# A list-scheduled two-layer block: new durations in the scheduler, and weight loads further ahead in the transfer queue

## The chip, the cores and the metric

The kernel runs on one core of a Trainium2 chip. The metric is device time in microseconds of one execution. The core's engines are TensorE (PE, matmuls; its weight loads are a row of their own, PEld), VectorE (DVE), ScalarE (ACT), GpSimd (POOL) and SyncE (SP), which here does nothing but issue all transfers (DMAs) in one order. Each engine executes its own instructions strictly in the order of the program.

## The reference, cut to what matters

Two layers over 1024 latent tokens and 256 context tokens, width 1024. In each, a conditioning vector gives scale, shift and gate (`w_ada`, 1024 x 3072), the normalised input goes through one projection (`w_in`, 1024 x 3600), four head groups work on slices of it, and an output projection closes the layer. The context shares the weights and feeds the latents only through the final states of the DeltaNet scan.

```python
for l in range(DEPTH):                                   # 2
    mod = silu(c) @ w_ada[l] + b_ada[l]                  # shift, scale, gate; the same with c_ctx
    h  = rmsnorm(x,  norm_g[l]) * (1 + scale) + shift
    hc = rmsnorm(xc, norm_g[l]) * (1 + scale_c) + shift_c
    if l % 2 == 1: h = to_col_major(h)
    p, pc = h @ w_in[l], hc @ w_in[l]                    # last layer: context needs group A only
    o_ctx, s_f, s_b = gdn_bidir(pc[..., :A_COLS], 0, 0, ...)
    o_lat, _, _     = gdn_bidir(p[..., :A_COLS], s_f, s_b, ...)
    y = mixer_output(o_lat, p, ...) # norm, conv3, conv31 + LayerNorm, spatial gate; each times silu(gate)
    x = x + gate * (y @ w_out[l])   # the context likewise in layer 0
return rmsnorm(x, final_g)
```

`gdn_bidir` works in chunks of 64 tokens: pair matrices of a chunk, the inverse of a triangular matrix, then a scan over chunks in both directions that carries a 64 x 64 state for each of 4 heads.

## The kernel before

**Dense work.** Each fp32 product is made of three matmuls in a rounded type (`mm3`): the weight tile is split into a high part (ScalarE CAST, `w<-r` or `u<-r`) and a low part (VectorE TENSOR_TENSOR `w<-r,w`), the input likewise (`hh`, `hl`). A projection takes 128 output columns at a time: 24 matmuls of 512 latent columns (or 256 context columns) fill one PSUM bank `mm`, of which there are three; an eviction then frees it. `dense` (its inner function `pump`) runs the pipeline of weights: load a raw tile `r` (512 KB, two buffers), split it, use it. While a raw tile is not yet split its buffer is taken.

**The program is recorded, then ordered.** All calls go to `Program.record` and `add`, which give each operation its dependences, an estimated duration (`estimate`; for a transfer a constant on SP), and a priority: its place in the recorded program plus the current `boost` (smaller is earlier). `schedule` then runs through estimated time and gives each engine, whenever it is free, the ready operation with the smallest priority; that fixes every engine's order, SP's too. Operations given with two engines (`either`: evictions, casts and scale-and-shift on ScalarE or VectorE) get their engine there, by which would be done first. So a changed duration moves instructions on all engines and from one engine to the other, though the set of operations stays the same. Priority offsets already exist: the scan stands 800 places ahead (`AHEAD_SCAN`), the splits in `pump` 600 (`AHEAD_SPLIT`), the DeltaNet preparation 300.

**Stages of the time.** The start: `c` arrives, eight `w_ada` tiles of 1 MB (`whh`, `whl`) feed the modulation, after each second one a slice of the context's `hh`, `hl` is ready (0 to 43 us). Then layer 0: context projections mixed with the making of the latents' `hh0` (to 164 us), latent projections, the context scan, the latent scan (440 to 590 us), the output projection with layer 1's `hh1`, token tile by token tile (690 to 810 us). Layer 1: projections, the context's inverse and scan (960 to 1000 us), the latents' pair matrices and inverse, the latent scan (1110 to 1200 us), the output projection. Of the names below, `mm` are dense PSUM banks, `sc` and `ax` other PSUM banks, `u`, `b`, `g` general buffers, `x` residual tiles, `zd`, `at` and `zb` scratch in memory through which pair matrices and inverses are reshuffled.

Of the kernel before, what the change touches and what calls it, by code (L numbers as in the profile page):

```python
# [79 lines left out]
class Program:  # L80
# [59 lines left out]
    def estimate(self, eng, method, out, ins, args, kw):  # L140
        acc = kw.get("accum_out") is not None
        n = max(self.cols(out), max([self.cols(x) for x in ins[:1]] or [0]))
        ps = any(str(x.space) == "MemoryType.PSUM" or "PSUM" in str(x.space) for x in ins)
        ptr = sum(1 for x in ins if self.cols(x) == 1) if n > 1 else 0
        if eng == "PE":
            if method == "transpose":
                return 0.218
            lhsT, rhs = ins[0], ins[1]
            n, m, k = self.cols(rhs), self.cols(lhsT), lhsT.shape[0]
            if "r" in str(rhs.dtype).split("float32")[-1]:  # L150
                return max(0.107, n / 2400.0 + 0.0133)
            if m <= 64 or k <= 64:
                return max(0.15, 0.05 + n * 4 / 2400.0) / self.side_by_side(k, m)
            return max(0.214, n * 4 / 2400.0) if n > 16 else 0.4
        if eng == "ACT":
            return (0.051 if ps else 0.093) + n / 1200.0 + 0.093 * (ptr + acc)
        if eng == "DVE":
            if method == "reciprocal":
                return 0.07 + n * 0.00625
            if method in ("tensor_scalar", "tensor_copy") and not ps:  # L160
                return 0.069 + n / 1920.0 + 0.06 * ptr
            return 0.069 + n / 960.0 + 0.06 * ptr
        if method == "memset":
            return 0.036 + n * 0.00083
        return 0.15 + n * 0.0021
# [20 lines left out]
    def add(self, calls):  # L186
        isap = lambda x: hasattr(x, "ap") and hasattr(x, "offset")
        eng, method, f, args, kw = calls[0]
# [18 lines left out]
        for e, m, fn, ar, k in calls:  # L207
            table = None
            if e == "ACT" and m == "activation":
                func = ar[2] if len(ar) > 2 else k.get("func")  # L210
                table = self.TABLE.get(str(func).split(".")[-1])
            o, n = aps(ar, k)
            cost = 0.475 if e == "SP" else self.estimate(e, m, o[0], n, ar, k)
            op.alts[e] = ((lambda fn=fn, ar=ar, k=k: fn(*ar, **k)), cost, table)  # L214
        deps, tiles = set(), set()
        for w, aps in ((False, ins), (True, outs)):
# [247 lines left out]
class Block:  # L464
# [357 lines left out]
    def dense(self, items):  # L822

        n = len(items)
# [3 lines left out]
        def pump(i):  # L828
            while True:
                s, moved = st["s"], False  # L830
                if s < min(i + 4, n) and s in raws:
                    it = items[s]
                    if self.room(it.pool)():
                        w = self.take(it.pool, [P, 2] + it.shape, F32R)
                        self.nc.boost -= AHEAD_SPLIT
                        self.split(w[:, 0], w[:, 1], raws.pop(s))
                        self.nc.boost += AHEAD_SPLIT
                        self.free("r")
                        ws[s] = w
                        st["s"] += 1  # L840
                        moved = True
                q = st["l"]
                if q < min(i + 6, n) and self.room("r")() and (items[q].cond is None or items[q].cond()):
                    raws[q] = r = self.take("r", [P] + items[q].shape)
                    items[q].load(r)
                    st["l"] += 1
                    moved = True
                if not moved:
                    return
# [1283 lines left out]
```

## Time and profile before

| | before |
|---|---|
| device time, median of 3 runs | 1384.58 us (1382.62 to 1386.99) |
| the profiled execution | 1382.8 us, its span 1381.1 us |
| mean granted TensorE clock | 0.969 of full |
| busy TensorE / VectorE / ScalarE | 1299.9 / 986.2 / 539.9 us (94 / 71 / 39%) |
| moved by transfers | 166.74 MB, mean 121 GB/s |

Busy time of TensorE is 94%, so some 81 us of the span are left in which it does nothing, and the clock of 0.969 says that in some stretches the granted clock was at the lower of its two levels (1.2 instead of 2.4 GHz). Both are spread unevenly, so the stage has to be looked at, not the mean.

### The profile page before, as it was taken

What the parts mean: (1) busy time and instruction counts of PE and PEld (TensorE: products, weight loads), DVE (VectorE), ACT (ScalarE), POOL (GpSimd) and SP (SyncE); (2) the same over time, 40 slices, a digit from 0 to 9 for tenths busy, and PEclk for the clock granted to TensorE, in tenths of its full rate; (3) what the DMA queues carried; (4) which work ended last, traced back from release to release, by engine and by line L of the source; (5) the groups of instructions that cost most, each with busy time, mean ns of one, the idle gap of its engine ahead of it and who ended that gap; (6) DMA issues with size and microseconds to landing.
All of it is one profiled execution on the core that took longest, in us unless ns stands there. A gap on an engine that the chain in (4) does not pass through costs nothing.

```text
span 1381.1 us, 27009 instructions
## 1 busy us (share of the span) xinstructions
PE 1299.9 (94%) x10992; PEld 1047.1 (76%) x10992; DVE 986.2 (71%) x2102; ACT 539.9 (39%) x903; POOL 11.9 (1%) x76
## 2 busy tenths in 40 slices
PE   6887899999999999999999999998999888999997
PEld 4886778987778666678887788987777776788886
DVE  3888959999869755753466659899788866753554
ACT  4877433254644221321244355343475121231221
POOL 1000000000000000000000000000000000000000
PEclk9988899999999999999999999999899989999999
DMA  9748232322485566561333341523237533122831
GB/s 306 213 109 242 58 74 70 86 47 61 111 203 145 151 198 190 185 184 54 109 115 111 100 113 51 128 54 88 66 99 178 121 80 100 49 76 96 269 82 56
DMA packets 308465, 166.74 MB, mean 121 GB/s; under 512 B 148254, under 2 KB 292982, under 8 KB 308342
## 3 DMA queue, kind: packets, MB, share of 16 engines
q1 hardware_dynamic: 308342, 165.03, 43.3%
q8 instruction: 86, 1.41, 0.4%
q14 instruction: 37, 0.30, 0.1%
HBM read 124.32 MB, written 35.42 MB: 116 GB/s over the span
## 4 chain that ended last, share of the span: by engine, by line
PE 60%; DVE 15%; DMA 14%; ACT 3%; issue 3%; SPq 3%; ACTq 0%; DVEq 0%
PE mm L214 45%; PE sc L214 11%; DVE u L214 8%; DMA x<-u 6%; PE ax L214 5%; DVE b L214 3%; SPq L214 3%; DMA r<-in_w_in 3%; DVE w L214 2%; DMA u<-in_w_out 2%; ACT u L214 1%; DMA whh<-in_w_ada 1%; DMA whl<-in_w_ada 1%; DMA u<-in_x 1%; DMA b<-zb 1%
## 5 line engine op out<-in xcount | busy, mean ns | idle before, releaser
L214 PE MATMUL mm<-hh,w 128*128 128x512 f32 x1664 | 541.4, 401 | 1.7 <-ACT w L214 1.2
L214 PEld LDWEIGHTS mm<-hh,w 128*128 128x128 f32 x1664 | 311.8, 190 | 82.0 <-issue 16.5
L214 PE MATMUL mm<-hl,w 128*128 128x512 f32 x832 | 334.3, 402 | 0.0
L214 PE MATMUL mm<-u,w 128*128 128x512 f32 (+1 forms) x1320 | 261.5, 356 | 1.6 <-ACT g L214 1.1
L214 PEld LDWEIGHTS mm<-u,w 128*128 128x128 f32 x1320 | 220.0, 193 | 35.3 <-ACT g L214 1.7
L214 DVE SCALAR_TENSOR_TENSOR u<-u,pv,u 128x1024 f32<-128x1024 f32 (+1 forms) x172 | 201.9, 1182 | 1.0
L214 PEld LDWEIGHTS mm<-hl,w 128*128 128x128 f32 x832 | 157.9, 190 | 40.7 <-issue 9.3
L214 ACT CAST w<-r 128x1024 fp32r<-128x1024 f32 x88 | 92.5, 1051 | 214.4 <-PE mm L214 159.2
L214 ACT ACT_TABLE_LOAD x94 | 120.6, 1283 | 17.7 <-DMA zd<-b 5.9
L214 DVE TENSOR_TENSOR w<-r,w 128x1024 fp32r<-128x1024 f32 x88 | 107.2, 1218 | 27.3 <-ACT w L214 26.8
L214 DVE TENSOR_TENSOR u<-u,b 128x256 f32<-128x256 f32 (+25 forms) x246 | 89.3, 378 | 26.5 <-DMA u<-in_x 16.3
L214 PE MATMUL mm<-u,u 128*128 128x256 f32 (+1 forms) x384 | 56.5, 299 | 9.8 <-ACT u L214 4.2
L214 DVE TENSOR_TENSOR b<-u 128x108 f32<-128x108 f32 (+21 forms) x180 | 56.5, 323 | 7.0 <-DMA u<-zd 3.8
L214 PEld LDWEIGHTS mm<-u,u 128*128 128x128 f32 x384 | 51.2, 200 | 12.8 <-DVE u L214 5.0
L214 ACT ACTIVATE b<-u 128x512 f32<-128x512 f32 (+1 forms) x71 | 42.5, 609 | 40.4 <-DVE u L214 29.4
L214 PEld LDWEIGHTS sc<-v,u 64*64 64x64 f32 x1184 | 40.3, 138 | 16.0 <-DVE v L214 9.9
L214 PEld LDWEIGHTS sc<-s,u 64*64 64x64 f32 x1168 | 40.6, 141 | 15.1 <-DVE s L214 4.5
L214 PE MATMUL sc<-s,u 64*64 64x64 f32 x1168 | 47.3, 230 | 2.3 <-DVE u L214 1.7
L214 PE MATMUL sc<-v,u 64*64 64x64 f32 x1184 | 46.6, 226 | 2.5 <-DVE v L214 1.3
L214 PE MATMUL mm<-u,hh 128*128 128x272 f32 x256 | 48.5, 289 | 0.0
L214 ACT ACTIVATE b<-sc,mod,modG 128x128 f32<-128x128 f32 x76 | 30.9, 459 | 44.5 <-PE sc L214 26.9
L214 PE MATMUL sc<-dg,u 128*128 128x128 f32 x248 | 38.2, 311 | 8.7 <-issue 4.7
(271 smaller groups left out, 1451.8 us busy)
## 6 DMA issues: line engine op xcount, KB each, us to landing
r<-in_w_in SPq DMA_DIRECT2D x90, 512.0 KB
u<-in_w_ada SPq DMA_DIRECT2D x16, 1024.0 KB
u<-in_x SPq DMA_DIRECT2D x16, 512.0 KB
r<-ylat SPq DMA_DIRECT2D x16, 512.0 KB
zd<-b SPq DMA_DIRECT2D x60, 128.0 KB
ylat<-g SPq DMA_DIRECT2D x24, 256.0 KB
u<-in_w_out SPq DMA_DIRECT2D x12, 512.0 KB
at<-b SPq DMA_DIRECT2D x36, 128.0 KB
```

The lines of the kernel that those rows point to most:

```text
L214: op.alts[e] = ((lambda fn=fn, ar=ar, k=k: fn(*ar, **k)), cost, table)
```

## The change

Two things. The table of durations in `estimate` is changed (transpose on TensorE; fixed part and pointer price on ScalarE; one-column, and two-input operations on 129 to 256 columns on VectorE; a transfer's issue on SP from 0.475 to 0.62). And the load of a raw weight tile gets the priority offset that its split already had, 600 places ahead. The whole diff:

```diff
--- before.py
+++ after.py
@@ -144,7 +144,7 @@
         ptr = sum(1 for x in ins if self.cols(x) == 1) if n > 1 else 0
         if eng == "PE":
             if method == "transpose":
-                return 0.218
+                return 0.11 if ins[0].shape[0] > 64 else 0.03
             lhsT, rhs = ins[0], ins[1]
             n, m, k = self.cols(rhs), self.cols(lhsT), lhsT.shape[0]
             if "r" in str(rhs.dtype).split("float32")[-1]:
@@ -153,10 +153,14 @@
                 return max(0.15, 0.05 + n * 4 / 2400.0) / self.side_by_side(k, m)
             return max(0.214, n * 4 / 2400.0) if n > 16 else 0.4
         if eng == "ACT":
-            return (0.051 if ps else 0.093) + n / 1200.0 + 0.093 * (ptr + acc)
+            return (0.155 if ps else 0.19) + n / 1200.0 + 0.05 * ptr + 0.093 * acc
         if eng == "DVE":
+            if n == 1:
+                return 0.155
             if method == "reciprocal":
                 return 0.07 + n * 0.00625
+            if method == "tensor_tensor" and not ps and 128 < n <= 256:
+                return 0.4
             if method in ("tensor_scalar", "tensor_copy") and not ps:
                 return 0.069 + n / 1920.0 + 0.06 * ptr
             return 0.069 + n / 960.0 + 0.06 * ptr
@@ -210,7 +214,7 @@
                 func = ar[2] if len(ar) > 2 else k.get("func")
                 table = self.TABLE.get(str(func).split(".")[-1])
             o, n = aps(ar, k)
-            cost = 0.475 if e == "SP" else self.estimate(e, m, o[0], n, ar, k)
+            cost = 0.62 if e == "SP" else self.estimate(e, m, o[0], n, ar, k)
             op.alts[e] = ((lambda fn=fn, ar=ar, k=k: fn(*ar, **k)), cost, table)
         deps, tiles = set(), set()
         for w, aps in ((False, ins), (True, outs)):
@@ -842,7 +846,9 @@
                 q = st["l"]
                 if q < min(i + 6, n) and self.room("r")() and (items[q].cond is None or items[q].cond()):
                     raws[q] = r = self.take("r", [P] + items[q].shape)
+                    self.nc.boost -= AHEAD_SPLIT
                     items[q].load(r)
+                    self.nc.boost += AHEAD_SPLIT
                     st["l"] += 1
                     moved = True
                 if not moved:
```

Helper lines move by four (218 in place of 214 is the line that issues every instruction). The order that comes out: TensorE and SP have the same instructions as before, 61 operations go over from ScalarE to VectorE and 21 the other way, and 5 of ScalarE's 94 function table loads are gone. Three places follow.

SP, the first transfers of the program (`r` are raw weight tiles, of which the first two are loaded in parts of 16 and 256 columns; `b_6` takes `c`, `whh` is the first half of `w_ada`'s tiles). Before:

```order
L214 DMA b_6_99<-in_c 8x128
L214 DMA b_6_99<-in_c_ctx 8x128
L214 DMA whh_104<-in_w_ada 128x8x256 x2
L214 DMA u_11_106<-in_ctx 128x1024 x2
L214 DMA whh_104<-in_w_ada 128x8x256
L214 DMA b_12_107<-in_norm_g 8x128
L214 DMA b_12_107<-in_b_ada 16x128
L214 DMA whh_104<-in_w_ada 128x8x256
L214 DMA b_12_107<-in_qkv_conv_w 18x128
```

With the change:

```order
L218 DMA r_39_134<-in_w_in 128x4x16
L218 DMA r_39_134<-in_w_in 128x4x256
L218 DMA r_41_136<-in_w_in 128x4x16
L218 DMA r_41_136<-in_w_in 128x4x256
L218 DMA b_6_99<-in_c 8x128
L218 DMA b_6_99<-in_c_ctx 8x128
L218 DMA whh_104<-in_w_ada 128x8x256 x2
L218 DMA u_11_106<-in_ctx 128x1024 x2
L218 DMA whh_104<-in_w_ada 128x8x256
L218 DMA r_43_138<-in_w_in 128x8x128
L218 DMA b_12_107<-in_norm_g 8x128
L218 DMA b_12_107<-in_b_ada 16x128
```

The loads of the first two weight tiles now stand ahead of `c`, and two further tiles (`r_43`, and `r_45` three rows on) between the `w_ada` loads, where they stood behind all of these.

VectorE, in layer 0, around the eviction of the dense bank `mm_264` (a context group whose last matmul ended at 118.2 us; `b_231` and `u_181` are the column-by-column inverse, `u_98` the 31-tap convolution, `rt`, `rs`, `dg` the norm of a latent token tile). Before:

```order
L214 TENSOR_TENSOR hl0_188<-b_252_349,hh0_187 128x4x128
L214 TENSOR_TENSOR b_231_328<-u_181_278 64x210
L214 TENSOR_TENSOR hl0_188<-b_256_353,hh0_187 128x4x128
L214 TENSOR_TENSOR u_181_278<-u_181_278,b_231_328 64x21x10
L214 RECIPROCAL rs_261_358<-rs_261_358 128x1
L214 SCALAR_TENSOR_TENSOR u_98_195<-u_98_195,pv0_73_168 128x256
L214 TENSOR_TENSOR b_231_328<-u_181_278 64x220
L214 TENSOR_TENSOR rt_262_359<-rs_261_358 128x1
L214 SCALAR_TENSOR_TENSOR u_98_195<-u_98_195,pv0_73_168 128x256
L214 TENSOR_TENSOR u_181_278<-u_181_278,b_231_328 64x20x11
L214 TENSOR_TENSOR rt_262_359<-rt_262_359,ss_258_355 128x1
L214 TENSOR_TENSOR u_52_147<-u_52_147,mm_264_361 128x256
```

With the change:

```order
L218 SCALAR_TENSOR_TENSOR u_98_195<-u_98_195,pv0_73_168 128x256
L218 TENSOR_TENSOR rs_261_358<-rs_261_358,rt_262_359 128x1
L218 TENSOR_TENSOR b_231_328<-u_181_278 64x240
L218 TENSOR_SCALAR dg_263_360<-ident_7_100,rs_261_358 128x128
L218 TENSOR_TENSOR u_181_278<-u_181_278,b_231_328 64x16x15
L218 SCALAR_TENSOR_TENSOR u_98_195<-u_98_195,pv0_73_168 128x256
L218 TENSOR_TENSOR b_231_328<-u_181_278 64x240
L218 SCALAR_TENSOR_TENSOR u_98_195<-u_98_195,pv0_73_168 128x256
L218 TENSOR_TENSOR u_181_278<-u_181_278,b_231_328 64x15x16
L218 TENSOR_TENSOR u_52_147<-u_52_147,mm_264_361 128x256
```

The same eviction stands 21 rows further down, behind ten more steps of the inverse and the norm of that token tile.

TensorE, in layer 1, just ahead of the first product of the context's inverse (`ax_1149`, `b_1133` to `b_1135` its operands; `mm_12..` are dense latent groups on `hh1`, `hl1`). Before:

```order
L214 MATMUL mm_1222_1321<-hh1_977,w_1215_1314 128x512 x2
L214 MATMUL mm_1222_1321<-hl1_978,w_1215_1314 128x512
L214 MATMUL mm_1222_1321<-hh1_977,w_1215_1314 128x512 x2
L214 MATMUL mm_1222_1321<-hl1_978,w_1215_1314 128x512
L214 MATMUL mm_1222_1321<-hh1_977,w_1215_1314 128x512 x2
L214 MATMUL ax_1149_1248<-b_1134_1233,b_1135_1234 32x32 x2
```

With the change:

```order
L218 MATMUL mm_1254_1353<-hh1_977,w_1219_1318 128x512 x2
L218 MATMUL mm_1254_1353<-hl1_978,w_1219_1318 128x512
L218 MATMUL mm_1254_1353<-hh1_977,w_1219_1318 128x512 x2
L218 MATMUL mm_1254_1353<-hl1_978,w_1219_1318 128x512
L218 MATMUL mm_1254_1353<-hh1_977,w_1219_1318 128x512 x2
L218 MATMUL mm_1254_1353<-hl1_978,w_1219_1318 128x512
L218 MATMUL ax_1149_1248<-b_1134_1233,b_1135_1234 32x32 x2
L218 MATMUL ax_1149_1248<-b_1133_1232,b_1135_1234 32x32 x2
```

The dense groups `mm_1222`, `mm_1240` and most of `mm_1254` now stand ahead of that product: 55 dense matmuls more than before.

## Rows read from the trace of the kernel before

**Rows 1.** The page, busy time of each engine: us, share of the span, instructions.

```profile
PE 1299.9 (94%) x10992; PEld 1047.1 (76%) x10992; DVE 986.2 (71%) x2102; ACT 539.9 (39%) x903; POOL 11.9 (1%) x76
```

**Rows 2.** Windows: length, busy us PE, PEld, DVE, ACT, POOL, clock, DMA share, GB/s.

```profile
0.00:40.00 40.00, 28.18 (x221) 19.53 (x221) 16.20 (x67) 16.64 (x36) 3.75 (x36) 1.00 0.98 309
40.00:60.00 20.00, 18.74 (x160) 17.92 (x160) 16.40 (x55) 17.68 (x33) 0.00 (x0) 1.00 0.60 173
60.00:80.00 20.00, 17.58 (x142) 17.12 (x140) 17.24 (x43) 16.58 (x34) 0.00 (x0) 0.83 0.56 147
80.00:100.00 20.00, 16.09 (x134) 15.02 (x133) 18.59 (x58) 14.42 (x26) 0.00 (x0) 0.91 0.54 143
100.00:120.00 20.00, 16.02 (x135) 15.14 (x134) 15.96 (x42) 16.30 (x32) 0.95 (x1) 0.91 0.74 197
120.00:140.00 20.00, 14.63 (x95) 12.85 (x94) 18.24 (x61) 13.72 (x30) 0.15 (x1) 0.80 0.79 226
140.00:160.00 20.00, 14.74 (x102) 14.20 (x102) 18.24 (x53) 11.93 (x25) 0.24 (x4) 0.78 0.16 40
840.00:940.00 100.00, 99.91 (x601) 87.41 (x600) 95.81 (x174) 45.64 (x72) 0.15 (x1) 1.00 0.37 86
940.00:960.00 20.00, 18.97 (x84) 15.39 (x82) 20.00 (x50) 6.57 (x9) 0.00 (x0) 1.00 0.28 66
960.00:1000.00 40.00, 36.99 (x516) 26.74 (x517) 31.18 (x53) 17.15 (x25) 0.95 (x1) 0.83 0.32 74
1100.00:1180.00 80.00, 66.19 (x1487) 52.84 (x1487) 54.04 (x132) 17.77 (x41) 0.00 (x0) 0.89 0.34 88
```

**Rows 3.** The chain that ended last, its transfers in the start: start, us, what.

```profile
4.86 10.79 DMA whh<-in_w_ada
...
17.09 8.31 DMA whl<-in_w_ada
...
29.53 7.98 DMA u<-in_x
```

**Rows 4.** Timeline of the start: start, us, instruction, idle before and its end.

```profile
7.21 1.94 PE L214 MATMUL sc<-whh,cs 128*32 128x256 f32 x16 [4.02 <-DMA whh<-in_w_ada]
...
31.74 1.10 ACT L214 CAST u<-r 128x1088 fp32r<-128x1088 f32 x1 [1.35 <-DMA r<-in_w_in]
```

**Rows 5.** Windows of 4 us in the start, when the first weight tiles are loaded.

```profile
24.00:28.00 4.00, 3.47 (x31) 1.82 (x23) 1.18 (x10) 2.08 (x4) 0.00 (x0) 1.00 0.99 282
28.00:32.00 4.00, 3.90 (x49) 2.20 (x51) 3.84 (x16) 1.59 (x5) 0.00 (x0) 1.00 1.07 298
```

**Rows 6.** The chain between 60 and 126 us, two of its transfers.

```profile
79.97 4.73 DMA r<-in_w_in
...
106.28 5.93 DMA r<-in_w_in
```

**Rows 7.** TensorE's waits from 40 to 160 us: total, times, longest.

```profile
PE ax L214 <- ACT b L214: 4.8, 2, 2.4
PE mm L214 <- DVE u L214: 4.0, 3, 2.9
PE mm L214 <- ACT u L214: 3.9, 1, 3.9
```

**Rows 8.** Timeline around the eviction of mm_264.

```profile
147.36 0.40 DVE L214 TENSOR_TENSOR u<-u,mm 128x256 f32<-128x256 f32 x1
...
147.82 2.29 PE L214 MATMUL mm<-u,u 128*128 128x256 f32 x9 [2.91 <-DVE u L214]
```

**Rows 9.** VectorE's instructions by form: count, busy us, mean ns, idle before.

```profile
L214 DVE TENSOR_SCALAR b<-sc,modG,mod 128x128 f32<-128x128 f32 x36 | 14.0, 401 | 7.0 <-ACT b L214 6.8
...
L214 DVE CAST hh<-b 128x256 fp32r<-128x256 f32 x15 | 6.2, 414 | 1.3 <-ACT b L214 0.3
```

**Rows 10.** Timeline of TensorE in layer 1, its two longest waits of that stretch.

```profile
963.01 1.20 PE L214 MATMUL ax<-b,b 32*32 32x32 f32 x64 [4.04 <-issue]
...
1104.79 1.19 PE L214 MATMUL ax<-b,b 32*32 32x32 f32 x64 [3.79 <-issue]
```

## The prediction, made before the changed kernel was run

> **What bounds the kernel now.** The page first: TensorE is busy 1299.9 us of 1381.1 [rows 1], so the kernel can only move where TensorE stands still, or runs at the lower clock, or is given the same work earlier. The windows say where that is [rows 2]. In the first 40 us it is busy 28.2, with the transfers at 309 GB/s and a share of 0.98: the start is bound by transfers. From 40 to 60 us it is busy 18.7 at full clock, so nearly bound by TensorE. From 60 to 160 us it is busy 17.6, 16.1, 16.0, 14.6 and 14.7 of 20, at clocks of 0.83 to 0.78, while VectorE is busy 16 to 18.6 and ScalarE 12 to 16.6: this stage hangs on chains through all three engines. From 940 to 1000 us the clock drops to 0.83 and TensorE waits 4.04 us [rows 2, 10]. From 1100 to 1180 us, the latent scan, it is busy 66.2 of 80. Nearly all else runs full.
>
> The chain of waits then says what ends those gaps. In the start it is queued transfers: a `w_ada` tile lands 10.8 and 8.3 us after the issue, an x tile 8.0 us after [rows 3]. From 60 to 126 us the chain passes twice through a raw weight tile whose load was issued late: at 79.97 and 106.28 us, landing 4.7 and 5.9 us on [rows 6]. Between 126 and 148 us it is VectorE's order: `mm_264` had ended at 118.2 us, its eviction ran at 147.36 us, and the next context group waited for that bank until 147.82 us [rows 8].
>
> **The change part by part. The start.** Two weight tiles of 544 KB each stand ahead of `c` now: 1.1 MB at 309 GB/s [rows 2] is 3.6 us, so the first `w_ada` matmul (7.21 us, after 4.02 us of waiting for its tile [rows 4]) comes 3.6 us later. Ahead of the last `w_ada` tile these two stood already; new there are `r_43` and `r_45`, 1.05 MB, 3.4 us. The context's last `hh` hangs on that tile, so 43 us becomes about 46. On the other side four weight tiles are split before they are needed: the first was cast at 31.74 us, 6 us after its issue [rows 4]. That gives TensorE a third dense group to fill its waits with, but only those between 28 and 44 us, some 1.5 us. I take 3.4 - 0.9 = **+2.5 us**; bounds +1.9 and +3.6. From 44 to 60 us TensorE is full, so weights that are ready sooner give nothing back there.
>
> Two of the moved loads are parts of 16 columns, 64 bytes a row. In the windows in which they are loaded the rate is 282 and 298 GB/s [rows 5], against 309 over the 40 us: 0.6 us in 8, which the bound above holds. The Trainium skill (DMA: Bandwidth & Descriptors, "Rules for kernel authors") says that transfers under 64 KB are mostly overhead, and its table of measured bandwidth gives 0.68 us for 4 KB and 0.95 us for 64 KB; an estimate from that page would put about 0.8 us for each 32 KB part at the head of the queue, and the term at +4 us in place of +2.5. The rows show a smaller loss than that.
>
> **Loads further ahead, 60 to 126 us.** On SP the loads after these stand one to fourteen places earlier; `r_213`, issued at 106.28 us, was behind sixteen shuffles of the inverse's operands that wait for VectorE, and now follows four. TensorE's waits in this stage are 4.8 us for ScalarE's `b`, 4.0 for VectorE's `u` and 3.9 for ScalarE's `u` [rows 7]. The last is one eviction queued behind a CAST that waited for the load issued at 79.97 us: it should go. The lower clock of 60 to 120 us is worth at most 0.17 + 0.09 + 0.09 of 20 us, 7 us [rows 2]. Bounds: nothing, and 3.9 plus half of the other idle time and of the clock (10 us). I take **-6 us**, nearer to the first wait than to the far end.
>
> **VectorE's order.** Ahead of the eviction of `mm_264` VectorE gets 23 operations that ScalarE had, and gives up 11: 12 more of about 0.41 us (0.40 to 0.41 in the two commonest forms [rows 9]) are 5.0 us. Ten steps of the inverse and three small operations that stood behind it stand ahead of it now: ten at 0.38 and 0.6 are 4.4 us. So it has 9.4 us more ahead of it, on an engine that is 91% busy from 120 to 160 us and idle for 13.6 us between 40 and 140 [rows 2]. If that idle time takes it all up, it costs nothing; if VectorE is the bound, 9.4 us. Behind the eviction waits `mm_295`, and behind that all of TensorE. The steps brought forward are not lost, since less is left behind; I take **+4 us**, the near half. From 160 us on TensorE is full for 240 us, so nothing of this is caught up there.
>
> **Layer 1.** The 55 dense matmuls that now stand ahead of `ax_1149` are 55 x 0.226 us (84 in 18.97 us from 940 to 960 [rows 2]) = 12.4 us: they fill the wait of 4.04 us [rows 10], and the context scan comes 8.4 us later. By itself that is a gain of 4.0 us and up to 0.17 x 40 = 6.8 of clock. But the latents' inverse hangs on that scan, and in turn the latent scan; TensorE waited for it 3.79 us at 1104.79 us [rows 10], with no dense work left ahead. What is gained at 963 us is waited for there, unless the chain between, with VectorE idle for some 9 us of 960 to 1000 [rows 2], is shortened. VectorE has about four more 0.4 us operations before it (1.6 us). Bounds: -10.8, and +7.3 (the chain rigid, 8.4 us late, less VectorE's slack of 1 us that is sure). I take **0**.
>
> **What costs nothing.** Five table loads fewer and the casts of `hh1` moved to VectorE: ScalarE is idle 61% [rows 1], and TensorE's order from 1200 us on is the same row by row. Cover for it is ScalarE's idle time; without it, 5 loads are 6.4 us.
>
> **The sum.** +2.5 - 6 + 4 + 0 = +0.5 us on 1382.8 us, the profiled execution's own time: 1383.3. The median of the runs is 1.8 us above that execution and the lowest run at its level; I take **1383 us**. A measurement here cannot tell less than 0.3%, 4.2 us, from no change.
>
> **The rivals.** *Faster: the waits go and nothing takes their place.* Start +2.5, early loads -8, the eviction at 0 because idle time takes it up, layer 1 at -4: -9.5, 1373 us; in a weaker form 1377. For it speaks that TensorE's largest single waits of 60 to 126 us follow late loads [rows 6, 7]; against it that VectorE, given more, is already at 91% [rows 2]. *Slower: the eviction decides.* If VectorE has no gap that the 9.4 us can use, the group `mm_295` starts that much later; with the start's 2.5 and early loads at -4 this is +8, 1391 us. It decides from where VectorE's idle time before 147 us falls below some 4 us. A second slower one is the latent scan at +7 with the rest at its value: 1390. *The change does not do what it says:* the order of the dense groups is the same throughout, so the loads may only be early and wait in their two buffers, SP standing still until a split frees one. Then start +2.5 and the eviction +2: 1387, just slower or the same.
>
> **How the numbers follow.** The forecast, all within 4.2 us of no change: 0.38, its own range 1379 to 1387. Faster in either form: 0.30. Slower by the eviction 0.15, by the latent scan 0.10, by the start alone (small rows, late `c`, nothing given back) 0.07: 0.32 together. The range of 8 in 10 goes from 1373 to 1392, the strong forms of both sides at its ends.
>
> **What would show it.** The first `w_ada` matmul at 10.5 to 11 us and the last slice of the context's `hh` near 46 us bear out the start; unchanged times refute it. The raw tile after the shuffles landing near 100 in place of 112 us, and no wait of 3.9 us near 82 us, bear out the early loads. The eviction of `mm_264`, and with it `mm_295`, at 147 to 152 us decides between the forecast and the rivals. In layer 1 the wait of 4.04 us must be gone, and the one before the latent scan longer by as much. The prediction is wrong if the scan's start moves by more than a few microseconds against that of the stage before, or if VectorE proves to have been waiting, not working, in 40 to 148 us.

## The result, and the profile after

The changed kernel takes 1398.9 us (median of 4 runs, 1396.19 to 1402.63) against 1383.7 us before (4 runs, 1382.62 to 1386.99): the ratio is 1.0108, 95% interval 1.0077 to 1.0138. It is slower by 15 us. The profiled execution of the changed kernel took 1398.07 us, its span is 1396.4 us, and all stage times below compare this one with the profiled execution of before.

The page of the changed kernel, busy time of each engine:

```profile
PE 1297.9 (93%) x10992; PEld 1043.8 (75%) x10992; DVE 993.1 (71%) x2142; ACT 517.9 (37%) x858; POOL 12.0 (1%) x76
```

TensorE does the same work as in [rows 1] in 2 us less of busy time, and the span is 15 us longer, so TensorE stands still 98.5 us in place of 81.2. VectorE has 40 instructions more. Windows of the changed kernel, the same stretches as in [rows 2], with one more (1100 to 1120 us) ahead of the last:

```profile
0.00:40.00 40.00, 20.39 (x159) 14.40 (x160) 16.88 (x62) 15.75 (x26) 3.84 (x36) 0.91 0.98 302
40.00:60.00 20.00, 19.42 (x177) 17.53 (x176) 14.92 (x56) 15.12 (x29) 0.00 (x0) 1.00 0.67 186
60.00:80.00 20.00, 18.15 (x173) 17.69 (x172) 19.25 (x53) 16.92 (x35) 0.00 (x0) 1.00 0.57 150
80.00:100.00 20.00, 15.78 (x137) 14.30 (x136) 18.50 (x58) 19.42 (x27) 0.00 (x0) 1.00 0.55 136
100.00:120.00 20.00, 15.15 (x113) 14.40 (x113) 18.43 (x42) 16.74 (x35) 0.00 (x0) 0.82 0.87 238
120.00:140.00 20.00, 17.07 (x119) 15.29 (x119) 15.90 (x59) 10.91 (x23) 1.05 (x2) 0.76 0.69 189
140.00:160.00 20.00, 11.63 (x64) 10.89 (x63) 18.48 (x56) 11.85 (x28) 0.33 (x4) 0.65 0.09 18
...
840.00:940.00 100.00, 99.34 (x629) 87.81 (x628) 97.77 (x169) 46.16 (x71) 0.35 (x5) 1.00 0.36 82
940.00:960.00 20.00, 20.00 (x90) 16.57 (x89) 18.39 (x41) 6.76 (x10) 0.00 (x0) 1.00 0.34 82
960.00:1000.00 40.00, 39.93 (x400) 30.98 (x398) 35.82 (x66) 18.40 (x27) 0.00 (x0) 1.00 0.29 70
...
1100.00:1120.00 20.00, 9.45 (x42) 7.50 (x40) 19.34 (x67) 1.06 (x1) 0.00 (x0) 0.83 0.29 70
1100.00:1180.00 80.00, 59.68 (x1157) 47.26 (x1157) 59.25 (x162) 15.69 (x33) 0.00 (x0) 0.86 0.38 93
```

The same window holds partly other work, since the changed kernel is up to 18 us late. Three stretches show most of the loss against [rows 2]: the first 40 us (28.18 to 20.39 us busy), 140 to 160 us (14.74 to 11.63), and 1100 to 1180 us (66.19 to 59.68). Two show a gain: 960 to 1000 us, now full and at full clock (36.99 to 39.93), and 40 to 80 us.

The start, timeline of TensorE and of ScalarE's first split (the first and the third line answer to [rows 4]):

```profile
11.40 1.93 PE L218 MATMUL sc<-whh,cs 128*32 128x256 f32 x16 [2.38 <-DMA whh<-in_w_ada]
...
34.50 0.43 PE L218 MATMUL sc<-ident,b 117*128 117x117 f32 x1 [3.97 <-DMA b<-in_gdn_norm_g]
...
6.75 1.10 ACT L218 CAST u<-r 128x1088 fp32r<-128x1088 f32 x1
```

The first weight tile is split at 6.75 us in place of 31.74, and the first `w_ada` matmul comes 4.2 us later. What the prediction had not counted is the second line: TensorE waits 3.97 us for the small vectors, whose last transfer (`gdn_norm_g`) was issued at 28.58 us in place of 20.29, behind all four weight tiles. In the kernel before, the same transfer and the same matmul, which had no wait:

```profile
20.29 0.55 SPq L214 DMA_DIRECT2D b<-in_gdn_norm_g  x2
...
27.77 0.32 PE L214 MATMUL sc<-ident,b 117*128 117x117 f32 x1
```

In the queue of the changed kernel:

```profile
25.89 2.35 SPq L218 DMA_DIRECT2D b<-in_conf_ln_g  x1
28.28 0.25 SPq L218 DMA_DIRECT2D b<-in_conf_ln_b  x1
28.58 0.55 SPq L218 DMA_DIRECT2D b<-in_gdn_norm_g  x2
```

The window of 4 us in which the first two raw tiles now arrive, narrow parts of the kind of [rows 5] among them:

```profile
4.00:8.00 4.00, 0.00 (x0) 0.00 (x0) 1.11 (x6) 2.38 (x2) 0.46 (x8) 1.00 1.07 324
```

It runs at 324 GB/s, above the mean of the start [rows 2] but below the 355 and 387 GB/s of the two windows of 4 us behind it: by these numbers an estimate of 0.5 us is lost in it. Further on, the raw tile that answers to the second row of [rows 6] was split at 98.35 us in place of 112.24. TensorE's waits from 40 to 160 us, in place of [rows 7]:

```profile
PE sc L218 <- DVE dg L218: 5.5, 1, 5.5
PE mm L218 <- ACT g L218: 4.6, 1, 4.6
PE mm L218 <- ACT u L218: 2.7, 3, 1.5
PE ax L218 <- ACT b L218: 2.5, 2, 2.1
```

The single wait of 3.9 us for ScalarE's `u` is gone; a wait of 5.5 us for VectorE's `dg` (the norm of a latent tile) is new. It stands just ahead of the eviction of `mm_264`, which ran at 153.28 us (147.36 in [rows 8]), as the timeline of the changed kernel shows; `mm_295` follows:

```profile
151.66 3.78 PE L218 MATMUL sc<-dg,u 128*128 128x128 f32 x16 [5.45 <-DVE dg L218]
153.28 0.41 DVE L218 TENSOR_TENSOR u<-u,mm 128x256 f32<-128x256 f32 x1
155.03 3.96 PEld L218 LDWEIGHTS mm<-u,u 128*128 128x128 f32 x24
```

The two forms of [rows 9] keep their durations on VectorE; there are 13 more casts of `hh`:

```profile
L218 DVE TENSOR_SCALAR b<-sc,modG,mod 128x128 f32<-128x128 f32 x38 | 14.8, 406 | 8.0 <-ACT b L218 8.0
...
L218 DVE CAST hh<-b 128x256 fp32r<-128x256 f32 x28 | 9.5, 413 | 0.5
```

In layer 1 the wait at 963 us [rows 10] is gone, and the one ahead of the latent scan is 13.58 us in place of 3.79:

```profile
1123.03 1.19 PE L218 MATMUL ax<-b,b 32*32 32x32 f32 x64 [13.58 <-issue]
```

To add this up, the end of the last matmul of the same bank was taken in both traces, at five places by which TensorE has the same work behind it in both: 273.6 us of before (`mm_402`; layer 0's context groups and latent `hh` are made), 596.8 (`mm_806`; latent scan of layer 0 over), 928.1 (`mm_1185`), 1106.0 (`ax_1319`, the product ahead of layer 1's latent scan), 1210.9 (`mm_1423`; that scan over). The changed kernel is late there by 2.6, 9.2, 9.7, 18.2 and 15.3 us, and nothing is added behind the last. So four stages cost +2.6, +6.7, +0.5, +8.5 and one gives back 2.9.

Two of these can be told more closely. The +6.7 us arise in the latent scan: at 450.1 us of before (`mm_655`, again with the same work behind it) the changed kernel is late by only 1.1 us. Around 500 us TensorE stands still for more than 5 us longer, in many waits of which none is over 1.7 us, and at a lower granted clock; before, then changed:

```profile
480.00:520.00 40.00, 39.49 (x763) 25.65 (x761) 20.71 (x48) 7.88 (x18) 0.00 (x0) 1.00 0.70 203
```
```profile
480.00:520.00 40.00, 34.19 (x647) 22.04 (x643) 21.43 (x53) 6.90 (x18) 0.00 (x0) 0.87 0.56 165
```

Of the +8.5 us, 6.3 are there when VectorE starts the latents' pair matrices (its first operation on `b_1226`, at 997.8 us of before), and 2.2 arise on the way from there to the last operation of their inverse (on `b_1317`).

### The profile page after: what moved, and what is told of

Read it like the earlier page. It is cut to its first block, busy times and chain, and to the rows that moved or that the text cites. A ratio compares the mean times of both kernels' runs of the same rounds, so it can differ in the third digit from the quotient of the medians.

```text
span 1396.4 us, 27023 instructions
## 1 busy us (share of the span) xinstructions
PE 1297.9 (93%) x10992; PEld 1043.8 (75%) x10992; DVE 993.1 (71%) x2142; ACT 517.9 (37%) x858; POOL 12.0 (1%) x76
## 5 line engine op out<-in xcount | busy, mean ns | idle before, releaser
L218 PEld LDWEIGHTS mm<-hh,w 128*128 128x128 f32 x1664 | 312.1, 189 | 85.1 <-issue 13.6
L218 DVE TENSOR_TENSOR b<-u 128x228 f32<-128x228 f32 (+24 forms) x180 | 56.2, 325 | 9.3 <-DMA u<-zd 7.7
L218 PE MATMUL mm<-u,u 128*128 128x256 f32 (+1 forms) x384 | 52.9, 292 | 0.9 <-ACT u L218 0.9
L218 PE MATMUL sc<-dg,u 128*128 128x128 f32 x248 | 37.9, 306 | 10.8 <-DVE dg L218 8.2
```

## The experiments

In the table, "ahead" counts dense matmuls in TensorE's order: ahead of the product that ends the latents' inverse in layer 0 (`ax_552`), ahead of the context inverse's product in layer 1 (`ax_1149`), and ahead of the end of the context scan (`sc_1229`). The five stage columns come from one profiled execution each, in us against that of before (in `l4_split300` and `inv300_conv0` 9 and 20 dense matmuls fewer stand ahead of the fourth place than in the others); the median and the ratio from all runs of the kernel, with the runs of before on the same chip (for the changed kernel those above, for the others a median of 1386.3 to 1387.6 us). That execution of before took 1382.8 us, 3.5 to 4.8 us less than those medians. The five columns of a row add up to the distance of two executions, and they miss the difference of the medians by -2 to +13 us (most for `l4_split300`, `loads_only` and `new_layer0_l4`), so a single column is weak, and only what several kernels agree in is read from it. Each pair of expectations says what its theories are.

| kernel | ahead | to 274 | to 597 | to 928 | to 1106 | to 1211 | median us | ratio, 95% interval |
|---|---|---|---|---|---|---|---|---|
| before | 1655 / 3400 / 3468 | 0 | 0 | 0 | 0 | 0 | | |
| changed | 1688 / 3455 / 3518 | +2.6 | +6.7 | +0.5 | +8.5 | -2.9 | 1398.9 | 1.0108 [1.0077, 1.0138] |
| durations_only | 1685 / 3455 / 3518 | +0.4 | +3.1 | +0.7 | +8.9 | -1.4 | 1396.5 | 1.0080 [1.0054, 1.0107] |
| loads_only | 1603 / 3400 / 3468 | -0.4 | +17.6 | -0.1 | +2.7 | +1.2 | 1397.6 | 1.0067 [1.0035, 1.0099] |
| late_first4 | 1686 / 3455 / 3518 | -0.1 | -0.7 | +0.9 | +9.0 | +1.8 | 1394.0 | 1.0053 [1.0028, 1.0078] |
| inv300_conv0 | 1633 / 3336 / 3408 | +0.3 | +6.2 | +1.0 | +9.9 | -5.0 | 1398.5 | 1.0082 [1.0056, 1.0108] |
| l4_split300 | 1685 / 3350 / 3413 | +0.6 | +5.5 | +0.9 | +15.3 | +3.0 | 1400.0 | 1.0100 [1.0068, 1.0132] |
| just_dvett | 1648 / 3438 / 3518 | -5.5 | +1.8 | +0.4 | +11.5 | -1.8 | 1393.1 | 1.0042 [1.0024, 1.0060] |
| loads_first4 | 1621 / 3400 / 3468 | -4.9 | +9.1 | +0.1 | +2.0 | +1.5 | 1390.6 | 1.0020 [1.0001, 1.0039] |
| loads_rest | 1630 / 3400 / 3468 | -1.9 | +9.2 | +0.3 | -1.4 | -1.0 | 1388.7 | 1.0020 [0.9998, 1.0043] |
| new_layer0 | 1688 / 3400 / 3468 | +3.3 | +9.0 | +0.3 | -1.1 | -2.0 | 1395.8 | 1.0066 [1.0044, 1.0087] |
| new_layer0_l4 | 1686 / 3400 / 3468 | +1.8 | 0.0 | +0.7 | +3.0 | -2.7 | 1382.2 | 0.9975 [0.9958, 0.9992] |
| new_layer1 | 1655 / 3455 / 3518 | -1.1 | +3.4 | +0.2 | +7.3 | -1.9 | 1393.9 | 1.0053 [1.0035, 1.0072] |
| dvett_layer0 | 1640 / 3400 / 3468 | -1.4 | +0.1 | +0.7 | +1.0 | +1.3 | 1383.3 | 0.9975 [0.9949, 1.0001] |
| loads_01 | 1604 / 3400 / 3468 | +2.1 | +7.3 | +0.6 | -1.0 | -0.7 | 1396.4 | 1.0077 [1.0054, 1.0100] |
| n0_ada | 1696 / 3400 / 3468 | +3.2 | +10.5 | +0.2 | +1.7 | +1.9 | 1400.9 | 1.0107 [1.0083, 1.0132] |
| d0_loads_rest | 1653 / 3400 / 3468 | -2.2 | -4.5 | -0.2 | -0.6 | -1.5 | 1373.5 | 0.9909 [0.9890, 0.9927] |

**The halves.** `durations_only` is the kernel before with the new table (and the 0.62 for a transfer), `loads_only` the kernel before with the three lines in `pump`.

> The changed kernel without the offset on the weight loads. Theory A: the start as before, the latent scan of layer 0 some 8 us late and that of layer 1 some 7 us more, because 30 and 55 dense matmuls stand ahead of their chains as in the changed kernel: 1394 to 1400 us, ratio 1.008 to 1.013. Theory B: within 4 us of the kernel before, 1380 to 1388 us.

> The kernel before with the offset on the weight loads alone, durations as before. Theory A (the durations are the loss: they put 33 dense matmuls more ahead of the latent scan of layer 0 and 55 ahead of the context scan of layer 1; this kernel has 52 fewer and the same number there): the start is late by about 10 us and given back by 100 us, both scans come no later, the whole 1376 to 1386 us, ratio 0.995 to 1.002. Theory B (the loads are the loss, because the start is late and nothing makes up for it): 1393 to 1399 us, most of the change's 15 us.

Both halves lose by themselves, and their losses do not add up. The durations bring the loss of layer 1 (+8.9 us), as theory A says; the loads bring one in layer 0 (+17.6 in this execution, the longest of its six), which it excluded.

**The first four loads at their old place**, and **other offsets** for the inverse and the convolution, both edits of the changed kernel:

```diff
-                    self.nc.boost -= AHEAD_SPLIT
+                    ahead = AHEAD_SPLIT if q >= 4 else 0      # late_first4
+                    self.nc.boost -= ahead                    # and += ahead behind the load
```
```diff
-..., AHEAD_INV, AHEAD_CONV, ... = ..., 0, 600, ...
+..., AHEAD_INV, AHEAD_CONV, ... = ..., 300, 0, ...            # inv300_conv0
```

> The changed kernel, but the first four weight loads have no offset and so stand behind c, the w_ada tiles and the vectors again. Theory A: the start is on time again (first w_ada matmul at 7.2 in place of 11.4 us, the context's last hh at 43 in place of 52 us), but since TensorE had made up for that by 100 us, the end moves by at most 3 us: 1394 to 1400 us. Theory B: 1384 to 1390 us, the start's 10 us come off the end.

> The changed kernel with two other priority offsets: the inverse 300 places further ahead (0 before), the 31-tap convolution at its own place (600 ahead before). In the order that comes out 1633 in place of 1688 dense matmuls stand ahead of the latent scan's inverse product in layer 0, 3336 in place of 3455 ahead of the context's in layer 1. Theory A (what matters is how much dense work is left when the scans run): the latent scan of layer 0 starts some 10 us earlier and that of layer 1 some 15 us or more earlier than in the changed kernel, the dense work goes into the scans, the whole 1370 to 1388 us. Theory B: no change beyond 3 us against the changed kernel, 1396 to 1402 us, since TensorE has the same work and the start is late.

`late_first4` is the changed kernel without its loss of layer 0: the 9 us of its fourth column arise in layer 1. Its median stands at the lower end of theory A, which had not expected layer 0 to gain. `inv300_conv0` puts 64 dense matmuls fewer than before (119 fewer than the changed kernel) ahead of the context's product, and that product did come 3.3 us earlier than before against its stage, but the stretch from the first operation of the latents' pair matrices to the last of their inverse took 116.3 us in place of 106.2: the order of VectorE had changed in it too. So it misses theory A's time by 10 us and more, and changes too much at once to decide on the mechanism.

**The order of TensorE or VectorE's list?** `l4_split300` is `late_first4` with `AHEAD_SPLIT` at 300; `just_dvett` is the kernel before with one entry of the table:

```diff
+            if method == "tensor_tensor" and not ps and 128 < n <= 256:
+                return 0.4                                    # just_dvett
```

> The version with the first four weight loads left at their old place, and the priority offset of the splits (and of the other loads) halved from 600 to 300. Ahead of the context inverse's product of layer 1 stand 3350 dense matmuls on TensorE (before 3400, changed kernel 3455), but VectorE still has some 11 us more of work ahead of the operation that this product waits for than before (changed kernel 20 us). Theory A (the order on TensorE makes the chain of layer 1 late, and the chain is rigid up to the latent scan): the stage from 930 to 1106 us costs 0 to +3 us against before in place of +9, and the time is 1384 to 1390 us. Theory B (VectorE's longer list ahead of the chain makes it late): the stage still costs +6 to +12, with TensorE waiting ahead of the product, and the time is 1392 to 1398 us.

> The kernel before with a single entry of the change: two-input VectorE operations on 129 to 256 columns at 0.4 us. TensorE gets 38 dense matmuls more ahead of the context inverse's product of layer 1 and 50 more ahead of the end of its scan (changed kernel 55 and 50), VectorE has nothing more ahead of it (-1.6 us). Theory A (order on TensorE): 930 to 1106 us costs +4 to +8 us, 1388 to 1396 us in all. Theory B (VectorE's list): 930 to 1106 us costs 0 to +2, and the time is within 0.3% of before, 1382 to 1390 us.

`l4_split300` fits neither theory: a split came too late, and TensorE waited for it with the whole of its order behind. Its waits from 930 to 1000 us:

```profile
PE mm L218 <- DVE w L218: 14.3, 1, 14.3
```

In `just_dvett` VectorE has nothing more ahead of the chain, TensorE 38 and 50 dense matmuls more, and the stage costs +11.5 us, more than theory A's 4 to 8. Of these, 4.7 us are there when the latents' pair matrices start, and that part is not from VectorE's list. The other 6.7 arise between there and the inverse's last operation (112.9 us in place of 106.2), with VectorE idle for 22.9 us in place of 14.9 and its order changed as well; what made that stretch longer is not shown. TensorE's timeline ahead of the latent scan in this kernel:

```profile
1112.98 1.19 PE L216 MATMUL ax<-b,b 32*32 32x32 f32 x64 [19.23 <-issue]
```

**Layer by layer.** In `new_layer0` the changed kernel goes back to the durations of before once layer 0's last output tile is recorded; `new_layer0_l4` also leaves the first four loads at their place; `new_layer1` is the kernel before with the new durations from there on; `dvett_layer0` the kernel before with only the entry of 0.4, and the 0.62 for a transfer with it, up to there. Each engine's order is so separated by layers: `ahead` in the table is that of one parent in layer 0 and of the other in layer 1, but for `dvett_layer0`, where the 0.62 makes 1640 of the 1648 of `just_dvett`.

```diff
-            cost = 0.62 if e == "SP" else self.estimate(e, m, o[0], n, ar, k)
+            new = self.era == 0                               # new_layer1: == 1
+            cost = (0.62 if new else 0.475) if e == "SP" else (self.estimate_new if new else self.estimate_old)(e, m, o[0], n, ar, k)
...
             if tt == 9:
+                nc.era = 1
                 W.flag(lc1.hflag)
```

> The changed kernel, in which operations recorded after layer 0's last output tile get the durations of before. Layer 0's order is that of the change throughout, and in layer 1 the dense matmuls ahead of the context inverse's product are 3400 again, as before (changed kernel 3455), those ahead of the scan's end 3468. Theory A (the new durations make layer 1's chain late through the order): 930 to 1106 us costs -1 to +3 us in place of +8.5, 1387 to 1393 us in all. Theory B (layer 1 is late because of what layer 0's new order leaves behind on VectorE, whose list up to there is still 13 us longer than before): 930 to 1106 us still costs +6 or more, 1394 to 1400 us. Theory C (what is lost ahead of the latent scan is mostly given back in it, as 3 of 8.5 us were in the changed kernel): the gain is under 3 us, 1394 to 1397.

> The same with the first four weight loads at their old place: what is left of the change is layer 0's durations and the later loads further ahead. late_first4 stood at -0.7 us at 597 us, so theory A gives 1384 to 1389 us, no change against before within 0.3%; theory B 1391 to 1397 us.

> The kernel before, in which only operations recorded after layer 0's last output tile get the new durations; weight loads as before. Up to 810 us every engine's order is that of before; ahead of the context inverse's product of layer 1 stand 3455 dense matmuls, as in the changed kernel. Theory A: 0 up to 930 us within 1.5, the wait of 4.04 us at 963 us gone, TensorE waiting 12 to 20 us ahead of the latent scan, 930 to 1106 us +7 to +12, 1393 to 1399 us in all. Theory B: no more than +2 us in that stage, 1385 to 1390 us.

> The kernel before with the single entry of 0.4 us for two-input VectorE operations, in layer 0 alone. With that entry in both layers the profile stood at -3.3 us at 928 us and at +8.2 ahead of the latent scan. Theory A: -2 to -4 us to the end, 1382 to 1386 us, the first version of these that is not slower than before. Theory B: the loss of layer 1 stays, 1390 to 1395 us.

In layer 1 theory A holds in all four: the stage to 1106 us costs -1.1, +3.0 and +1.0 us with 3400 ahead, and +7.3 with 3455. All ten kernels with 3400 ahead, before among them, have the very same order on TensorE from 928 us to that product, and on VectorE from the latents' pair matrices to their inverse, so -1.4 to +3.0 us is what executions of one order differ by here. `new_layer1` shows the whole exchange: two windows of it, and its wait ahead of the latent scan in TensorE's timeline.

```profile
960.00:1000.00 40.00, 39.93 (x501) 30.74 (x501) 33.57 (x61) 17.32 (x25) 0.95 (x1) 1.00 0.30 65
...
1100.00:1120.00 20.00, 3.55 (x134) 3.16 (x135) 15.74 (x49) 2.78 (x6) 0.00 (x0) 0.54 0.40 106
```
```profile
1114.63 1.19 PE L246 MATMUL ax<-b,b 32*32 32x32 f32 x64 [17.49 <-issue]
```

At 960 to 1000 us it wins 2.9 us of busy time and all of the clock over [rows 2]; ahead of 1114.6 us it waits 17.5 us, with no dense work left ahead of that product in its order. Theory B falls, since layer 0's new order alone (`new_layer0`) costs nothing here, and theory C too: under 3 us come back in the scan, not most. What was wrong is the total of `new_layer0`, 1395.8 us against 1387 to 1393: layer 0 with the early first loads costs more than was thought, since leaving those four at their place is worth 13.6 us to the median here (6.6 between the two profiled executions).

Four kernels so have layer 0's new durations and the later loads ahead, and differ in two things. With neither the first four loads ahead nor layer 1's new durations (`new_layer0_l4`) the ratio is 0.9975; with the durations alone (`late_first4`) 1.0053, with the four loads alone (`new_layer0`) 1.0066, with both (the changed kernel) 1.0108. So these two make up the whole loss. By the ratios each costs somewhat less beside the other than alone, which the intervals leave open.

**What of the loads costs.** `loads_first4` and `loads_rest` give the offset to `q < 4` and to `q >= 4`, `loads_01` to `q < 2`, all on the kernel before. `n0_ada` is `new_layer0` with the offset around `ada_load` in `ada_rest` too.

> The kernel before, with the offset for the first four weight loads only: the start part of the change alone. In the profile of the changed kernel the start was 9.8 us late at 44 us and given back by 84 to 110 us. Theory S1 (given back, since TensorE has slack up to 160 us and the weights are ready): within 0.3% of before, 1382 to 1390 us, with +5 to +10 us at 44 us and under +3 at 274 us. Theory S2 (the start's loss stays): 1391 to 1396 us.

> The kernel before, with the offset for all weight loads but the first four. The start is unchanged; ahead of layer 0's last product before the latent scan stand 1630 dense matmuls (before 1655, with all loads ahead 1603). Theory L1 (all loads ahead lost 11 us because the shuffles of the latents' inverse wait on the transfer queue behind the loads, and TensorE stands still at 380 to 560 us): +6 to +12 us between 274 and 597 us, 1391 to 1398 us in all. Theory L2 (the loss came from the first four loads and the order that they bring about): within 0.3% of before, 1380 to 1389 us.

> The kernel before, with the offset for the first two weight tiles only: these stand ahead of c, the next two behind the small vectors (norm_g, b_ada, the convolution weights, gdn_norm_g), ahead of the last w_ada tile. So as many bytes stand ahead of the last w_ada tile as with four, 1.05 MB more than before, and only the vectors have 1.05 MB less ahead of them. Theory V (the start was 8 to 10 us late instead of 2.5 because all four tiles stand ahead of the small vectors, on which the modulation hangs): +3 to +5 us at 44 us in place of +8.1 for four. Theory W (the start hangs on the last w_ada tile, so on the bytes ahead of that one): +7 to +9 us at 44 us. To the end: no more than 0.3% from before if the start is given back, 1383 to 1391 us; +6 or more if the loss of layer 0 behind 274 us comes with the first two loads.

> The changed kernel with layer 1's durations of before, and with the offset of 600 places for the loads of the w_ada tiles of the background modulation too. In the version without this TensorE waited 2.9 us at 505 us for such a tile, and then 1.4 us for the scan's own chain; with the first four weight loads at their old place there was no such wait, and that version was 13.6 us faster. Theory M (the scan of layer 0 is held up by modulation tiles that the weight loads pushed back in the queue): no wait for w_ada in 460 to 600 us, 274 to 597 us costs +3 to +6 in place of +9, 1388 to 1393 us. Theory N (that wait is a small part, the rest is the clock and order around 420 to 440 us): gain under 3 us, 1392 to 1398.

At the start theory V holds. At 43.6 us of before (the context group `mm_54`) four early tiles cost +8.1 us (9.8 in the changed kernel), two only +3.7. There they have 14 to 31 matmuls more behind them; at 30.0 us (`sc_83`), with the same work behind it in all, it is +7.3 (8.4 in the changed kernel) against +2.9: the other 4.4 us come from the tiles ahead of the small vectors. Theory S1 holds as far as 274 us, where `loads_first4` is 4.9 us early, and its median lies just above the 1390 us that it allows. But behind that, to 597 us, the profiled execution of every version with loads ahead on the kernel before loses 7 to 18 us against that of before. `loads_01`, whose median is 10 us above before, shows that two early loads at the very start are enough for a loss. For `loads_rest` the medians do not bear it out: 1388.7 against 1387.6 us, with 1 inside the interval of the ratio. In `new_layer0` TensorE waits in layer 0's latent scan for a tile of the modulation:

```profile
505.42 0.90 PE L246 MATMUL ax<-u,cs 128*32 128x256 f32 x8 [2.91 <-DMA u<-in_w_ada]
```

This was taken as the cause, and `n0_ada` speaks against it: the wait shrank to 1.4 us, and the kernel is slower by 5 us, not faster. It misses both of its theories, and since the wait is not gone and the order is another one, it does not rule the cause out.

**The parts that do not lose, together.** `d0_loads_rest` is `dvett_layer0` (its 0.62 for a transfer in layer 0 included) with the offset for `q >= 4`.

> What the runs so far leave as the better half of the change: the single entry of 0.4 us in layer 0 alone, and the offset for all weight loads but the first four. Alone the entry gave 0.9975, the loads 1.002. If each acts by itself: 0.997 to 1.000 of before, 1382 to 1387 us. If, as for all loads with the whole table, two changes of the order meet badly in layer 0 between 376 and 597 us: 1389 to 1396.

It is better than expected: 0.9909 of before, all six runs (1371.47 to 1377.9 us) below the fastest of before on that chip (1381.57). Its window over layer 0's latent scan, behind that of before, and the longest of TensorE's waits of 274 to 460 us:

```profile
480.00:600.00 120.00, 117.94 (x1809) 77.38 (x1808) 71.79 (x158) 29.62 (x58) 0.20 (x4) 1.00 0.67 198
```
```profile
480.00:600.00 120.00, 118.77 (x1599) 77.43 (x1598) 73.06 (x152) 31.21 (x57) 0.20 (x4) 1.00 0.67 201
```
```profile
PE sc L244 <- ACT b L244: 0.4, 1, 0.4
```

TensorE is busy 118.77 of 120 us there, 117.94 before and 113.13 in the changed kernel. So the same two kinds of edit that cost 15 us can save 13 us (1386.3 less 1373.5) when another order comes out; what makes this order better is not shown.

## Why the prediction was wrong

Of the 15 us between the forecast and the measurement, layer 1 makes 5.6 (+8.5 less 2.9, against a term of 0), layer 0 from 274 us on 7.2 with what follows it (no term), and the start with the rest up to 274 us 2.1.

**Layer 1 is the step that failed.** The prediction had the mechanism and both ends of it: 55 dense matmuls fill the wait at 963 us, the context scan comes later, and "what is gained at 963 us is waited for there". Then it took 0, in the middle between -10.8 and +7.3, on the chance that the chain could be shortened. It was not. The context inverse's product came 8.4 us later against its stage, just as worked out, and the latents' pair matrices 6.3 us later. From their first operation to the last of their inverse it took 106.2 us before and 108.4 in the changed kernel, 110.0 in `durations_only`; the ten executions with the order of before took 104.3 to 109.8, so the 2.2 us may be no more than what executions differ by. The stage cost +8.5 us, just beyond the upper bound, and 2.9 came back in the scan: the scan's start moved against the stage before, which was the prediction's own sign of being wrong. All four kernels with 3455 ahead cost 7.3 to 9.0 us there, all nine others with 3400 from -1.4 to +3.0. At the start of the pair matrices the two kinds stand as far apart: 4.1 to 6.3 us late against -1.9 to +0.9. That separation is shown; the rival "latent scan at +7" had it, at a chance of 0.10. The count alone is not a law, since `l4_split300` and `inv300_conv0`, with fewer than 3400 ahead, lost more, by a wait for a split and by a longer stretch to the inverse's end (118.6 and 116.3 us).

**Layer 0's latent preparation and scan were not in the sum.** The stage from 274 to 597 us had no term, since TensorE was nearly full there. It cost +6.7 us. Two pairs of kernels that differ in the place of the first four loads alone (changed and `late_first4`, `new_layer0` and `new_layer0_l4`) stand 7.4 and 9.0 us apart in this stage, so the loss comes with these loads and the order that they bring about, long after they have landed. What stays open is how: halving the wait for a modulation tile did not help. Of the versions with 1603 to 1633 dense matmuls ahead of `ax_552` all lose 6 to 18 us, those with 1640 to 1655 stand between -4.5 and +3.4, and those with 1685 to 1696 between -0.7 and +10.5. A product placed too early makes TensorE wait for it, one placed too late delays the scan; that reading fits, but is argued, not shown, and the count does not decide it (1686 cost -0.7 and 0.0, 1688 +6.7 and +9.0).

**The start was mis-sized.** The term was +3.4 us for the context's last `hh`, less 0.9 that TensorE makes up. That slice came at 52.2 us in place of 42.8, 9.4 later. The step that failed is that two of the four tiles "stood already" ahead of the last `w_ada` tile: true, but the modulation waits for the small vectors too, and of these all four were behind. TensorE, with the same work behind it, was 8.4 us late at 30.0 us and 5.2 at 54.2 (`sc_127`): it made up for 3.2 in between with other work brought forward (31 matmuls more by `mm_54`, which is why it looks 9.8 late there). So the term of +2.5 (bounds 1.9 and 3.6) is 5.2. From there to 62.2 us (`sc_143`, +5.3) nothing is given back, as the prediction had it. The first `w_ada` matmul was 4.2 us late for 3.6 of bytes; the remaining 0.6 us is about what the rows of the narrow parts had said [rows 5] (0.5 in 8 when it is worked out again). The price that the Trainium skill would give (DMA: Bandwidth & Descriptors, "Bandwidth", a table for transfers issued from GpSimd) is 1.6 us for both parts, an estimate from that page; the trace shows less than half of it.

**Early loads and the eviction were about right.** From 62.2 us to `mm_210` at 90.8 us, where the changed kernel is 2.1 us early with the same work behind it, it wins 7.4 us, for a term of -6. Around the eviction of `mm_264`, from 144.9 us (`ax_277`, +1.3) to 157.7 (`mm_298`, +5.5), it loses 4.2, for a term of +4; what TensorE waits for is `dg`, which stands ahead of the eviction in VectorE's order, and the eviction came at 153.28 us, just outside the 147 to 152 that were to decide. Another 3.4 us lost between 90.8 and 144.9 had no term. At 164.2 us (`mm_316`) it is still 5.5 late, and 2.9 of that is caught up by 274 us, which the prediction excluded: it called TensorE full there, but it was idle for 4.2 us from 160 to 400 us in the trace of before. So the sum of these terms, +0.5, stands against +2.6 measured at 274 us, and most of the miss of 15 us lies behind it. The table loads (89 in place of 94) show no cost.

## What to carry to other kernels

A list schedule's durations are not judged by how near each is to the trace, but by where they put the chains: here a table nearer to the trace started a chain of layer 1 some 6 us late, nothing shortened the chain, and the stage lost 8.5 us; a single entry of the table was enough to start it 4.7 us late. When a change fills a wait with work that was to fill a later one, look at the end of the chain for what is left to do there; if nothing is, the wait has only moved, and the bound, not the middle, is the value to take. Prices of parts of such a change do not add, so try them by halves and stages: a part of this one (one duration of VectorE and that of a transfer, in layer 0 alone, and all weight loads ahead but the first four) took 0.9% less than before.

## What the hardware showed that was not expected

Two executions of one order differ by more than the stage effects that one would like to read: `new_layer1` has the order of before on every engine up to 597 us, and yet its profiled execution is 2.3 us later there, after being 1.1 us earlier at 274. In the stage of layer 1 up to 1106 us, ten executions of one order span 4.4 us. So a stage of one execution tells little below some 4 us.

What an idle time goes with can be more than its own length. In `new_layer0` TensorE stood still for 1.25 us, until 421.99 us, and the granted clock of the window from 420 to 440 us was 0.66, which is 13.6 of 20 us at the lower level. In `new_layer0_l4` the gap at the same place was 0.37 us, until 419.46, and the clock 0.91, which is 3.6 us. Two of the dense matmuls took 1.05 us together at the lower level and 0.62 at the upper one. The orders of the two differ, so that the longer gap is the cause is not shown. The windows of the two:

```profile
420.00:440.00 20.00, 18.75 (x178) 15.10 (x177) 12.59 (x43) 9.35 (x13) 0.16 (x1) 0.66 0.68 169
```
```profile
420.00:440.00 20.00, 20.00 (x193) 16.50 (x190) 14.67 (x52) 7.90 (x11) 0.16 (x1) 0.91 0.63 152
```
